# Compressed keys beside the selected branch's keys: one key tile, shared score matmuls, and the first loads in another order

## The chip, the cores and the metric

The kernel runs on one core of a Trainium2 chip. The metric is the device time in microseconds of one execution. A core has TensorE (PE in the rows; PEld is its weight loading), VectorE (DVE), ScalarE (ACT), GpSimd (POOL) and SyncE (SP, which here issues the DMAs). Each engine works through its own list of instructions in a fixed order, and waits on semaphores for the others.

## What is computed

One decoder layer on 1024 tokens of width 1024, in float32. One input projection feeds two groups of heads; their outputs are joined, projected, added to the input and normalised, and a SwiGLU feed-forward part with a second normalisation follows. The part that matters here is the sparse-attention group, with 8 heads in 2 key groups. Each head has three branches that share the query, and a gate weighs each branch's output:

```python
s_c = einsum('btghd,bngd->btghn', q, kc) * scale          # compressed: 63 keys, one per 16 tokens
p_cmp = masked_softmax(s_c, mask_c)                        # key n is seen from token 16 n + 31 on
o_cmp = einsum('btghn,bngd->btghd', p_cmp, vc)
...
s = einsum('bqghd,bqgkd->bqghk', q_blk, kg) * scale        # selected blocks of 64 tokens
s = s - slopes * dist                                      # linear distance penalty
p = masked_softmax(s, dist >= 0)
...
o = gates[..., 0:1] * o_cmp + gates[..., 1:2] * o_sel + gates[..., 2:3] * o_win
```

There are 16 blocks and 16 are selected, so the selected branch is plain causal attention over all keys up to the query. The window branch sees 512 tokens back.

## The kernel before

**Numbers.** A float32 operand is split into a high and a low part (`split`, lines 78 to 82: a cast on ScalarE, a subtraction on VectorE or GpSimd), and a product is three matmuls (`mm3`, lines 113 to 117). Score matmuls use another form: the 64 features of a head and their low part are stacked on the 128 rows, so that a score is two matmuls, with the high part of the query and then the low part as weights (L303, L304).

**Stages.** First the projections that the compressed branch and the selected branch's keys need (128 columns of `w_in` each, loaded as `w_t[0]`, `w_t[1]`, `w_t[2]`), with `x` transposed in eight tiles (`xT[hf, kp]`: token half `hf`, two of the eight 128-row blocks of the width in each). For each width block `k`, three `mm3` follow one another, one into each of three PSUM banks. Then queries, values, gates, and the compressed keys (`compress`, `compress_out`: the keys of group `g` land in a tile `kcc[g]` of 64 columns). Then attention: four phases, one for each pair of sparse heads (`nsa(0)` to `nsa(3)`), then phases of differential attention, then the output projection, the feed-forward part and the stores.

**A phase of a pair of heads** has 16 units: for each block `i` of 128 queries the selected branch (kind 0, `128 (i + 1)` keys) and the window branch (kind 1, up to 640 keys). A unit has a front and a back. The front makes the scores of both heads `a` (`scores`: pieces of at most 512 columns, each in one of the two banks of the PSUM tag S; VectorE reads a piece once, adds the distances, scales, and keeps the row minimum, L307), then exponentials on ScalarE with the sum of each row (L320), reciprocals (L400) and one multiplication by reciprocal and gate on GpSimd (L401). The back transposes the result on TensorE (L339), splits it, and multiplies by the values into the PSUM tag O (L408 for the compressed branch, L416 and L418 for the other two). The back of a unit comes after the front of the next one (`look` is 1), and pieces of later projections ("fillers") are put between.

**The compressed branch** is done for four blocks and both heads at once, in `cmp_front` (lines 357 to 380), at blocks 0 and 4 of each phase: 16 matmuls of 64 columns into one bank, a copy to SBUF, the causal mask by an affine select on GpSimd, minimum, subtraction, exponentials, sum, reciprocal and the gated multiplication, over a 128x512 tile `pc`.

**What sets the order.** The code is written against priorities (backs and fillers are put later, by `BACK_LATER` and `FILL_LATER`), and a scheduler that simulates the engines writes the fixed order of each engine's list when the kernel is built. DMAs leave SP's queue in order; a DMA that has to wait holds those behind it. SBUF tiles are named slots: slot 0 and slot 1 hold the keys of group 0 for the selected and the window branch, slots 6 and 7 those of group 1.

## Time and profile before

| | |
|---|---|
| runs timed | 1336.2, 1337.75, 1339.09 us; median 1337.75 us |
| the profiled execution | 1335.19 us, of which the span of the rows is 1333.5 us |
| TensorE busy | 1305.0 us, 98% of the span |
| VectorE, ScalarE, GpSimd busy | 918.9, 638.3 and 468.9 us |
| the four phases of sparse heads | 89.0 to 413.8 us of the span |

The span runs from the first to the last instruction of the program. Matmuls overlap in the rows (one of 512 columns shows some 0.4 us, and the next starts 0.23 us after it), so what a matmul costs is read from the starts of neighbours, not from its length.

### The profile page before, as it was taken

The page shows a single profiled execution, that of the slowest core. Times are in us where ns is not written, and L with a number is a line of the kernel's source. Part 1 is how long each engine was busy: PE and PEld are TensorE (multiplying, and loading weights), DVE is VectorE, ACT ScalarE, POOL GpSimd, SP SyncE. Part 2 cuts the span into 40 slices and gives each one's busy share as a digit, 9 for nine tenths or more (in the row PEclk, how much of TensorE's full clock was granted, in tenths as well). Part 3 has the DMA queues.
Part 4 walks back from the last instruction along what each step waited for, and adds up shares of the span by engine and source line. Part 5 has one row for each costly group of instructions (what it writes and reads, how often), then busy time and mean ns, then how long its engine had stood idle before and what let it go on. Part 6 is the DMA issues. An engine that isn't in the chain of part 4 may idle for free.

```text
span 1333.5 us, 20339 instructions
## 1 busy us (share of the span) xinstructions
PE 1305.0 (98%) x7018; PEld 1116.4 (84%) x7018; DVE 918.9 (69%) x1882; ACT 638.3 (48%) x1293; POOL 468.9 (35%) x464
## 2 busy tenths in 40 slices
PE   8999999999999998999999999999999999999997
PEld 6898998888888887878878888888888888888886
DVE  5546767868799456675687668777677777555587
ACT  5336676767787447653345233333333335533330
POOL 5415354453455336554522233223213232000072
PEclk9999999999999999999999999999999999999999
DMA  9411021120211215523212656555455549868541
GB/s 348 140 29 50 19 61 48 31 62 24 62 33 46 72 48 159 181 96 118 103 64 81 219 192 242 180 181 190 156 201 182 190 158 317 291 202 286 192 173 63
DMA packets 86695, 183.12 MB, mean 137 GB/s; under 512 B 10560, under 2 KB 19136, under 8 KB 86464
## 3 DMA queue, kind: packets, MB, share of 16 engines
q1 hardware_dynamic: 86592, 181.82, 41.4%
q8 instruction: 55, 0.90, 0.3%
q14 instruction: 48, 0.39, 0.1%
HBM read 116.18 MB, written 57.15 MB: 130 GB/s over the span
## 4 chain that ended last, share of the span: by engine, by line
PE 88%; DVE 4%; DMA 3%; ACT 1%; issue 1%; POOL 1%; SPq 0%; POOLq 0%; DVEq 0%; ACTq 0%
PE psM L115 10%; PE psM L117 10%; PE psM L116 10%; PE psT L117 6%; PE psT L115 6%; PE psT L116 6%; PE psS L117 6%; PE psS L115 6%; PE psS L116 5%; PE psT L339 4%; PE psS L303 3%; PE psS L304 3%; PE psO L418 2%; PE psO L472 2%; PE psO L416 2%; PE psO L117 2%
## 5 line engine op out<-in xcount | busy, mean ns | idle before, releaser
L320 ACT ACTIVATE t<-t,m 128x128 f32<-128x128 f32 (+7 forms) x192 | 144.2, 752 | 73.6 <-DVE m L307 69.0
L401 POOL TENSOR_SCALAR t<-t,r,gates 128x640 f32<-128x640 f32 (+7 forms) x128 | 100.0, 783 | 152.0 <-DVE r L400 104.0
L115 PE MATMUL psM<-big,w 128*128 128x512 f32 x304 | 121.4, 399 | 2.0 <-ACT w L80 2.0
L117 PE MATMUL psM<-big,w 128*128 128x512 f32 x304 | 121.1, 399 | 0.0
L116 PE MATMUL psM<-big,w 128*128 128x512 f32 x304 | 120.2, 396 | 0.0
L303 PE MATMUL psS<-slot,q 128*128 128x320 f32 (+5 forms) x288 | 106.4, 372 | 7.4 <-DVE m L307 5.4
L971 POOL TENSOR_TENSOR half<-half,half 128x512 f32<-128x512 f32 x22 | 33.3, 1515 | 198.7 <-ACT half L970 198.7
L82 DVE TENSOR_TENSOR pt<-psT,pt 128x512 fp32r<-128x512 f32 (+1 forms) x152 | 91.5, 613 | 12.4 <-ACT pt L80 11.5
L304 PE MATMUL psS<-slot,q 128*128 128x320 f32 (+5 forms) x288 | 95.2, 333 | 0.0
L307 DVE CUSTOM_DVE_ANT_0 t<-psS,dsel 128x512 f32<-128x512 f32 (+5 forms) x128 | 67.7, 535 | 34.1 <-PE psS L304 30.2
L80 ACT CAST pt<-psT 128x512 fp32r<-128x512 f32 (+1 forms) x152 | 76.8, 527 | 26.5 <-PE psT L339 14.1
L82 DVE TENSOR_TENSOR op<-op 128x1024 fp32r<-128x1024 f32 x44 | 60.7, 1385 | 38.9 <-ACT op L80 35.7
L339 PE MATMUL psT<-ident,t 128*128 128x128 f32 x528 | 83.8, 273 | 1.5 <-DVE pt L82 1.3
L82 DVE TENSOR_TENSOR big<-slot,big 128x1024 fp32r<-128x1024 f32 (+1 forms) x53 | 65.3, 1239 | 27.6 <-ACT big L80 27.5
L80 ACT CAST big<-slot 128x1024 fp32r<-128x1024 f32 (+1 forms) x53 | 54.0, 1034 | 61.6 <-DVE slot L963 55.2
L80 ACT CAST op<-op 128x1024 fp32r<-128x1024 f32 x44 | 45.9, 1051 | 65.2 <-DMA op<-t_d 57.2
L418 PE MATMUL psO<-pt,slot 128*128 128x256 f32 x264 | 73.2, 298 | 0.7 <-DVE pt L82 0.6
L975 POOL TENSOR_TENSOR half<-half,half 128x512 f32<-128x512 f32 x22 | 36.4, 1657 | 101.8 <-DVE half L974 101.7
L416 PE MATMUL psO<-pt,slot 128*128 128x256 f32 x264 | 71.7, 289 | 0.6 <-ACT pt L80 0.6
L303 PEld LDWEIGHTS psS<-slot,q 128*128 128x128 f32 x288 | 54.4, 189 | 17.7 <-DVE m L307 12.9
L339 PEld LDWEIGHTS psT<-ident,t 128*128 128x128 f32 x528 | 62.5, 140 | 7.7 <-issue 1.4
L115 PEld LDWEIGHTS psM<-big,w 128*128 128x128 f32 x304 | 57.2, 188 | 12.6 <-ACT w L80 2.7
(372 smaller groups left out, 3957.0 us busy)
## 6 DMA issues: line engine op xcount, KB each, us to landing
a_d<-slot SPq DMA_DIRECT2D x77, 256.0 KB, 3.1
t_d<-slot SPq DMA_DIRECT2D x77, 256.0 KB, 2.3
q<-q SPq DMA_DIRECT2D x48, 256.0 KB, 3.0
slot<-in_w_up_dram SPq DMA_DIRECT2D x22, 512.0 KB, 3.9
slot<-in_w_down_dram SPq DMA_DIRECT2D x22, 512.0 KB, 3.9
op<-a_d SPq DMA_DIRECT2D x44, 256.0 KB, 3.1
op<-t_d SPq DMA_DIRECT2D x44, 256.0 KB, 3.8
big<-a_d SPq DMA_DIRECT2D x33, 256.0 KB, 2.9
```

What stands on the lines that cost most here:

```text
L80: nc.scalar.copy(hi, src)
L82: eng.tensor_sub(lo, src, hi.bitcast(F32))
L115: nc.tensor.matmul(acc, lhsT=ah, rhs=bh, start=first, stop=False, skip_group_check=more)
L116: nc.tensor.matmul(acc, lhsT=ah, rhs=bl, start=False, stop=False, skip_group_check=more)
L117: nc.tensor.matmul(acc, lhsT=al, rhs=bh, start=False, stop=last, skip_group_check=more)
L303: nc.tensor.matmul(ps[:, :w], lhsT=q[0], rhs=k[:, ks], start=True, stop=False)
L304: nc.tensor.matmul(ps[:, :w], lhsT=q[1], rhs=k[:, ks], start=False, stop=True)
L320: nc.scalar.activation(t[:, :width], t[:, :width], AF.Exp, bias=m, scale=-1.0, accum_out=r)
L339: nc.tensor.transpose(tp[:rows, n * P:(n + 1) * P], s, ident)
L401: nc.gpsimd.tensor_scalar(ts[a][:, :width], ts[a][:, :width], r[:, a:a + 1], gates[:, i, gc:gc + 1], op0=ALU.mult, op1=ALU.mult)
L416: nc.tensor.matmul(po[:, :256], lhsT=v, rhs=pt[:, 0, n * 256:(n + 1) * 256], start=False, stop=False)
L418: nc.tensor.matmul(po[:, :256], lhsT=v, rhs=pt[:, 1, n * 256:(n + 1) * 256], start=False, stop=last)
```

## The change

1. The compressed keys no longer have a tile of their own. The key tile of the selected branch (slots 0 and 6) grows from 1024 to 1088 columns; the first 64 hold the compressed keys. `cmp_front` goes. In a selected unit the first score piece covers the 64 compressed keys and the first part of the selected keys, with the same two matmuls.
2. VectorE reads that first piece twice: 64 columns with a new distance tile `dcmp` (zero, or huge where the key is not yet to be seen), the rest as before. The compressed softmax is now done for each unit and head: an exponential over 64 columns, four reciprocals in one instruction, one multiplication on GpSimd.
3. Pieces are cut anew: `n` pieces for 64 + width columns, in multiples of 32. Block 3 (576 columns) now has two pieces instead of one, and block 7 (1088) three instead of two.
4. The first loads are cut in halves and put in the order in which the first matmuls take them, and the low parts of the first halves of all three weights are made on VectorE.

```diff
@@ scores @@
-            n = (width + 511) // 512
-            w = width // n
+            c = NC if cmp else 0
+            n = (c + width + 511) // 512
+            w = -(-(c + width) // (32 * n)) * 32
+            part, at = width - (n - 1) * w, 0
+            m0 = None
             for h in range(n):
                 ps = ps_s()
-                ks = slice(k0 + h * w, k0 + (h + 1) * w)
-                nc.tensor.matmul(ps[:, :w], lhsT=q[0], rhs=k[:, ks], start=True, stop=False)
-                nc.tensor.matmul(ps[:, :w], lhsT=q[1], rhs=k[:, ks], start=False, stop=True)
...
+                ks = slice(k0 + at, k0 + at + part + c)
+                nc.tensor.matmul(ps[:, :c + part], lhsT=q[0], rhs=k[:, ks], start=True, stop=False)
+                nc.tensor.matmul(ps[:, :c + part], lhsT=q[1], rhs=k[:, ks], start=False, stop=True)
+                if c:
+                    k0 += c
+                    nc.vector.tensor_tensor_reduce(out=cmp[0], in0=ps[:, :c], in1=cmp[1], scale=slope, scalar=3.0e38,
+                                                   op0=ALU.add, op1=ALU.min, accum_out=cmp[2])
+                m1 = m if h == n - 1 else pa.tile([P, 1], F32, tag="m0", name="m0", bufs=4)
+                nc.vector.tensor_tensor_reduce(out=t[:, at:at + part], in0=ps[:, c:c + part],
+                                               in1=dist[:, at:at + part], scale=slope,
                                                scalar=3.0e38 if h == 0 else m0, op0=ALU.add, op1=ALU.min,
-                                               accum_out=m if h == n - 1 else m0)
+                                               accum_out=m1)
+                at, part, c, m0 = at + part, w, 0, m1
@@ nsa_units @@
-            def cmp_front(hf):
...
                 def front():
-                    if i % 4 == 0 and kind == 0:
-                        cmp_front(i // 4)
...
                     for a in range(2):
-                        scores(q_of(qt, i, a), K[kind], j0 * P, width, dist, sl[a], m[:, a:a + 1], ts[a])
-                        exps(ts[a], width, m[:, a:a + 1], r[:, a:a + 1])
+                        ms, rs = ([t[:, n:n + 1] for n in (a, 2 + a)] for t in (m, r))
+                        cmp = (pc[:, a, :], dcmp[:, 56 - 8 * i:56 - 8 * i + NC], ms[1]) if kind == 0 else None
+                        scores(q_of(qt, i, a), K[kind], j0 * P, width, dist, sl[a], ms[0], ts[a], cmp)
+                        exps(ts[a], width, ms[0], rs[0])
+                        if kind == 0:
+                            exps(pc[:, a, :], NC, ms[1], rs[1])
+                    nr = 2 if kind else 4
+                    nc.vector.reciprocal(r[:, :nr], r[:, :nr])
                     for a in range(2):
-                        gc = heads[a] * 3 + 1 + kind
-                        nc.vector.reciprocal(r[:, a:a + 1], r[:, a:a + 1])
-                        nc.gpsimd.tensor_scalar(ts[a][:, :width], ts[a][:, :width], r[:, a:a + 1],
-                                                gates[:, i, gc:gc + 1], op0=ALU.mult, op1=ALU.mult)
+                        for n, t in ((1 + kind, ts[a][:, :width]), (0, pc[:, a, :] if kind == 0 else None)):
+                            if t is not None:
+                                gc = heads[a] * 3 + n
+                                c = a if n else 2 + a
+                                nc.gpsimd.tensor_scalar(t, t, r[:, c:c + 1], gates[:, i, gc:gc + 1],
+                                                        op0=ALU.mult, op1=ALU.mult)
@@ the first loads @@
-        for k in range(2):
-            cs = slice(k * 512, (k + 1) * 512)
-            nc.sync.dma_start(raw_x[:, cs], xT[0, 0][:, cs])
-            nc.sync.dma_start(raw_w[:, cs], w_t[0][:, cs])
-            for raw, t in ((raw_x, xs[0, 0]), (raw_w, w3[0])):
-                split(raw[:, cs], t[0][:, cs], t[1][:, cs])
-        w3.append(load_split(w_t[1], *w_tiles(), land=slot(8, F32), l_eng="pool", pieces=2))
-        w3.append(load_split(w_t[2], t_tile(), t_tile(), land=slot(9, F32), l_eng="pool", pieces=2))
...
+        piece(xT[0, 0], raw_x, xs[0, 0], 0)
+        for n in range(3):
+            piece(w_t[n], raw_w[n], w3[n], 0)
+        piece(xT[0, 0], raw_x, xs[0, 0], 1)
+        load_x(0, 1, 2)
+        for n in range(3):
+            piece(w_t[n], raw_w[n], w3[n], 1, "pool" if n else "dve")
```

`piece` loads one half of a tile and splits it.

The first DMAs in SP's list, before (128x512 is half of a tile):

```order
L663 DMA slot_107<-in_xT_dram 128x512
L664 DMA w<-in_w_t_dram 128x512
L663 DMA slot_107<-in_xT_dram 128x512
L664 DMA w<-in_w_t_dram 128x512
L89 DMA slot_125<-in_w_t_dram 128x512 x2
L89 DMA slot_134<-in_w_t_dram 128x512 x2
L89 DMA slot_142<-in_xT_dram 128x1024
```

and after:

```order
L663 DMA slot_106<-in_xT_dram 128x512
L663 DMA w<-in_w_t_dram 128x512
L663 DMA slot_114<-in_w_t_dram 128x512
L663 DMA slot_115<-in_w_t_dram 128x512
L663 DMA slot_106<-in_xT_dram 128x512
L92 DMA slot_132<-in_xT_dram 128x512 x2
L663 DMA w<-in_w_t_dram 128x512
L663 DMA slot_114<-in_w_t_dram 128x512
L663 DMA slot_115<-in_w_t_dram 128x512
```

The first halves of the second and third weights move from places 5 and 7 to places 3 and 4, the second half of the first `x` tile from 3 to 5, and the next `x` tile comes ahead of the second halves of all weights.

TensorE's list at the end of the first `cmp_front`, before (`kcc0` are the compressed keys of group 0, `q_458` and `q_459` the queries of the two heads, `slot0` the selected keys):

```order
L365 MATMUL psS_843<-kcc0_86,q_459 128x64
L366 MATMUL psS_843<-kcc0_86,q_459 128x64
L303 MATMUL psS_876<-slot0_230,q_458 128x128
L304 MATMUL psS_876<-slot0_230,q_458 128x128
L116 MATMUL psM_923<-big_171,q_406 128x512
```

and after, at the same place:

```order
L313 MATMUL psS_854<-slot0_236,q_464 128x192
L314 MATMUL psS_854<-slot0_236,q_464 128x192
L313 MATMUL psS_861<-slot0_236,q_465 128x192
L314 MATMUL psS_861<-slot0_236,q_465 128x192
L119 MATMUL psM_905<-big_173,q_412 128x512
```

The matmuls of 64 columns are gone, and those of block 0's selected keys have 192 columns instead of 128. In the whole list there are 96 matmuls fewer.

VectorE's list in the selected unit of block 7 of the first phase, before (rows ending in 128x1 read the minimum out; `psS_1740` and `psS_1745` are the two banks of the first head):

```order
L307 ISA t_1738,m0_1743<-psS_1740,dsel_90 128x512
L307 ISA m0_1743 128x1
L400 RECIPROCAL r_1645<-r_1645 128x1
L424 TENSOR_TENSOR tmp_1639<-psO_1506,tmp_1639 64x256
L82 TENSOR_TENSOR pt_1685<-psT_1680,pt_1685 128x512
L82 TENSOR_TENSOR pt_1700<-psT_1695,pt_1700 128x512
L307 ISA t_1738,m_1736<-psS_1745,dsel_90,m0_1743 128x512
```

and after:

```order
L317 ISA pc_1729,m_1725<-psS_1730,dcmp_90 128x64
L317 ISA m_1725 128x1
L320 ISA t_1727,m0_1734<-psS_1730,dsel_88 128x256
L320 ISA m0_1734 128x1
L393 RECIPROCAL r_1635<-r_1635 128x2
L422 TENSOR_TENSOR tmp_1629<-psO_1490,tmp_1629 64x256
L360 TENSOR_TENSOR pt_1665<-psT_1662,pt_1665 64x256
L320 ISA t_1727,m0_1739<-psS_1736,dsel_88,m0_1734 128x384
L320 ISA m0_1739 128x1
L85 TENSOR_TENSOR pt_1674<-psT_1669,pt_1674 128x512
L85 TENSOR_TENSOR pt_1689<-psT_1684,pt_1689 128x512
L320 ISA t_1727,m_1725<-psS_1741,dsel_88,m0_1739 128x384
```

The first bank is now read by two instructions before it is free, and the head's scores come in three pieces instead of two.

## Rows read from the trace of the kernel before

**Rows 1.** The page, part 1: busy time, share of the span, instructions.

```profile
PE 1305.0 (98%) x7018; PEld 1116.4 (84%) x7018; DVE 918.9 (69%) x1882; ACT 638.3 (48%) x1293; POOL 468.9 (35%) x464
```

**Rows 2.** Busy time by stretch: PE, PEld, DVE, ACT, POOL, clock, DMA share, GB/s.

```profile
5.80:15.10 9.30, 6.70 (x24) 3.96 (x24) 4.48 (x5) 6.39 (x9) 8.08 (x23) 1.00 1.00 363
15.10:89.00 73.90, 73.90 (x448) 65.87 (x446) 36.47 (x74) 26.36 (x72) 21.23 (x18) 1.00 0.45 162
89.00:171.50 82.50, 81.65 (x559) 74.83 (x559) 58.05 (x186) 50.25 (x125) 32.47 (x39) 1.00 0.15 38
171.50:252.00 80.50, 79.38 (x554) 71.51 (x552) 60.48 (x198) 57.64 (x140) 37.90 (x44) 1.00 0.18 47
252.00:332.00 80.00, 78.72 (x513) 70.18 (x511) 58.95 (x183) 54.31 (x130) 36.81 (x43) 1.00 0.18 47
332.00:413.80 81.80, 79.87 (x562) 71.58 (x560) 70.34 (x237) 64.05 (x157) 38.75 (x48) 1.00 0.20 50
```

**Rows 3.** Waits of PE and PEld, 89 to 414: total us, times, longest.

```profile
PE psS L303 <- DVE m L307: 2.2, 6, 0.6
...
PEld psS L303 <- DVE m L307: 6.3, 16, 1.1
```

**Rows 4.** PE in order of time from 252 us: start us, length us, instruction.

```profile
253.06 0.28 PE L366 MATMUL psS<-kcc,q 128*128 128x64 f32 x1
...
254.51 0.37 PE L418 MATMUL psO<-pt,slot 128*128 128x256 f32 x1
...
255.30 0.39 PE L115 MATMUL psM<-big,w 128*128 128x512 f32 x1
...
257.14 0.40 PE L117 MATMUL psM<-big,w 128*128 128x512 f32 x1
```

**Rows 5.** What uses the tile pc: length ns min/median/max, first and last start.

```profile
L374 ACT ACTIVATE pc<-pc x16: 402/410/441, 92.5 to 376.3; 128x256 f32<-128x256 f32 x16
L368 ACT COPY pc<-psS x8: 567/586/588, 89.2 to 371.2; 128x512 f32<-128x512 f32 x8
...
L371 DVE TENSOR_REDUCE cst<-pc x8: 677/686/689, 90.6 to 373.8; 128x8 f32<-128x512 f32 x8
...
L375 DVE TENSOR_REDUCE cst<-pc x8: 628/682/687, 93.8 to 377.9; 128x8 f32<-128x512 f32 x8
```

**Rows 6.** Groups by form, 80 to 420: busy us, mean ns | idle before.

```profile
L320 ACT ACTIVATION_READ_ACCUMULATOR t<-t,m 128x1 f32 x136 | 25.8, 190 | 0.0
L400 DVE RECIPROCAL r<-r 128x1 f32<-128x1 f32 x128 | 20.0, 158 | 14.2 <-ACT t L320 12.6
...
L307 DVE DVE_READ_ACCUMULATOR2_ANT m<- 128x1 f32 x201 | 16.3, 81 | 0.0
...
L320 ACT ACTIVATE t<-t,m 128x256 f32<-128x256 f32 x18 | 9.1, 509 | 10.6 <-DVE m L307 10.6
...
L320 ACT ACTIVATE t<-t,m 128x128 f32<-128x128 f32 x18 | 7.2, 402 | 10.6 <-DVE m L307 10.4
L401 POOL TENSOR_SCALAR t<-t,r,gates 128x128 f32<-128x128 f32 x16 | 7.1, 447 | 18.5 <-DVE r L400 16.1 <-DVE gates L718 1.7 <-PE psT L339 0.6
...
L307 DVE CUSTOM_DVE_ANT_0 t<-psS,dsel 128x128 f32<-128x128 f32 x10 | 2.8, 287 | 3.1 <-PE psS L304 2.5 <-PE psT L339 0.5
```

**Rows 7.** ACT in order of time, start: the casts that end a load.

```profile
7.67 0.62 ACT L80 CAST w<-w 128x512 fp32r<-128x512 f32 x1 [1.33 <-DMA w<-in_w_t_dram]
...
9.19 0.62 ACT L80 CAST w<-slot 128x512 fp32r<-128x512 f32 x1 [0.25 <-DMA slot<-in_w_t_dram]
```

**Rows 8.** PE in order of time, start.

```profile
5.80 0.77 PE L115 MATMUL psS<-big,w 128*128 128x512 f32 x1
...
12.98 0.50 PE L115 MATMUL psS<-big,w 128*128 128x512 f32 x1 [0.74 <-ACT big L80]
```

**Rows 9.** PE in order of time, 530.9 to 536.2.

```profile
531.05 0.30 PE L303 MATMUL psS<-slot,q 128*128 128x128 f32 x1 [1.69 <-DMA q<-q]
```

**Rows 10.** Busy time by stretch, as in group 2, after that wait.

```profile
532.00:536.00 4.00, 4.00 (x24) 4.00 (x22) 0.71 (x5) 0.77 (x4) 0.73 (x2) 0.57 0.68 169
```

More of the change, by code (lines that the diff above doesn't have):

```diff
@@ L25 @@
 NCMP = 63
+NC = NCMP + 1
 WIN_BLOCKS = 5
@@ L62, in ps_m, with slot @@
         return psum.tile([P, 512], F32, tag="M", name="psM", bufs=2)
-    def slot(n, dt=F32R):
-        return slots.tile([P, 1024], dt, tag=f"slot{n}", name=f"slot{n}", bufs=1)
+    def slot(n, dt=F32R, wide=False):
+        w = 1024 + NC if n in (0, 6) else 1024
+        t = slots.tile([P, w], dt, tag=f"slot{n}", name=f"slot{n}", bufs=1)
+        return t if wide or w == 1024 else t[:, :1024]
     def w_tile(dt=F32R):
@@ L184, in layer_kernel @@
         pes = const.tile([P, 2, 16], F32, name="pes")
-        kcc = [const.tile([P, 64], F32R, name=f"kcc{g}") for g in range(2)]
         vcc = [const.tile([P, P], F32R, name=f"vcc{g}") for g in range(2)]
@@ L224, in compress_out @@
                 for g in range(2):
[L225 to L227 removed]
+                    kc = KC[g][:, :NC]
+                    nc.scalar.copy(kc[0:64, :], op[0:64, g * 64:(g + 1) * 64])
+                    nc.vector.tensor_sub(kc[64:128, :], op[0:64, g * 64:(g + 1) * 64], kc[0:64, :].bitcast(F32))
             else:
@@ L251, in layer_kernel @@
         dwin = pa.tile([P, 640], F32, tag="dwin", name="dwin", bufs=1)
+        dcmp = pa.tile([P, NC + 56], F32, tag="dcmp", name="dcmp", bufs=1)
         qscale = pa.tile([P, 12], F32, tag="qscale", name="qscale", bufs=1)
@@ L294, in q_of, with scores @@
             return q[:, c:c + P], q[:, 512 + c:512 + c + P]
[L296 to L299 removed]
+        def scores(q, k, k0, width, dist, slope, m, t, cmp=None):
+            c = NC if cmp else 0
[3 more added lines that the diff above has]
+            m0 = None
             for h in range(n):
                 ps = ps_s()
[L302 to L308 removed]
+                ks = slice(k0 + at, k0 + at + part + c)
[8 more added lines that the diff above has]
+                                               in1=dist[:, at:at + part], scale=slope,
                                                scalar=3.0e38 if h == 0 else m0, op0=ALU.add, op1=ALU.min,
[L310 removed]
+                                               accum_out=m1)
+                at, part, c, m0 = at + part, w, 0, m1
         def t_tiles(width):
@@ L355, in nsa_units @@
             state = {}
-            def cmp_front(hf):
-                pc = pa.tile([P, 2, 4, 64], F32, tag="pc", name="pc", bufs=2)
-                ps = ps_s()
-                for a in range(2):
-                    for i4 in range(4):
-                        q = q_of(qt, hf * 4 + i4, a)
-                        o = ps[:, (a * 4 + i4) * 64:(a * 4 + i4 + 1) * 64]
-                        nc.tensor.matmul(o, lhsT=q[0], rhs=kcc[g], start=True, stop=False)
-                        nc.tensor.matmul(o, lhsT=q[1], rhs=kcc[g], start=False, stop=True)
-                st = small([P, 3, 2, 4], "cst", 2)
-                nc.scalar.copy(pc.rearrange("p a i n -> p (a i n)"), ps)
-                nc.gpsimd.affine_select(pc, pc, pattern=[[0, 2], [P, 4], [-16, 64]], base=hf * 512 - 31,
-                                        channel_multiplier=1, compare_op=ALU.is_ge, fill=BIG)
-                nc.vector.tensor_reduce(st[:, 0], pc, axis=AX.X, op=ALU.min)
-                nc.gpsimd.tensor_sub(pc, pc, st[:, 0].unsqueeze(3).to_broadcast([P, 2, 4, 64]))
-                for a in range(2):
-                    nc.scalar.activation(pc[:, a], pc[:, a], AF.Exp, scale=-sl[a])
-                nc.vector.reduce_sum(st[:, 1], pc, axis=AX.X)
-                nc.vector.reciprocal(st[:, 1], st[:, 1])
-                gc = gates[:, hf * 4:hf * 4 + 4, 6 * p:6 * p + 6].rearrange("p i (a c) -> p a i c", c=3)[:, :, :, 0]
-                nc.vector.tensor_mul(st[:, 2], st[:, 1], gc)
-                nc.gpsimd.tensor_mul(pc, pc, st[:, 2].unsqueeze(3).to_broadcast([P, 2, 4, 64]))
-                state[hf] = pc
             def make(i, kind):
@@ L406, in back @@
                         state["po"] = po = ps_o()
-                        ptc = transposed([state[i // 4][:, a, i % 4, :] for a in range(2)], rows=64)
+                        ptc = transposed([ts[2][:, a, :] for a in range(2)], rows=64)
                         nc.tensor.matmul(po[:, :256], lhsT=vcc[g], rhs=ptc[:, 0, :256], start=True, stop=False)
```

35 lines of the change are left out of this document (20 added, 15 removed).

## The prediction

> **What bounds the kernel now.** I read the page's first part first: TensorE is busy for 98% of the span [rows 1]. So a change here is worth what it takes off TensorE's list, or off the few waits in it; work on another engine counts only where TensorE comes to wait for it. Then the busy times by stretch [rows 2], which say where such waits are. From 15.10 to 89.00 us TensorE is busy for all 73.90 us. In the four phases of sparse heads it is busy for 319.6 of 324.8 us (sum of the four rows), while VectorE is busy for 247.8, ScalarE for 226.3 and GpSimd for 145.9. In the first 9.30 us after the first real matmul it is busy for 6.70, with DMA at 1.00. Third, the waits of TensorE in the phases [rows 3]: the largest is a score matmul or its weight load that waits for VectorE to free a bank of tag S, 6 and 16 times, 2.2 and 6.3 us. That is the wait which the change can feed.
>
> **The change part by part.**
>
> *Matmuls taken away.* `cmp_front` runs twice in each of four phases, 16 matmuls each, 128 in all. Their cost is their spacing: from the one at 253.06 to the matmul behind the last at 254.51 there are 13 steps in 1.45 us, 0.1115 us each [rows 4]. 128 x 0.1115 = 14.3 us.
>
> [...]
>
> *Columns given back.* The same 64 columns now ride on the selected units' matmuls. Eight 512-column matmuls take 257.14 - 255.30 = 1.84 us [rows 4], 0.23 us each, so 64 columns cost 0.23/8 = 0.029 us if cost goes with columns. 4 phases x 8 blocks x 2 heads x 2 matmuls = 128 times 0.029 = 3.7 us. For block 0 (128 becomes 192 columns) the cost may be nothing, since 64 columns with their weight load already take 0.11; that takes at most 0.5 off, and I take 3.4.
>
> *Pieces added.* Blocks 3 and 7 get one piece more: 2 blocks x 4 phases x 2 heads x 2 = 32 matmuls more, with no more columns. 128 - 32 = 96 fewer, as the lists say. The pieces have at least 256 columns, whose stream at 0.23 us for 512 is 0.115 us and so covers the 0.11 us that a weight load sets [rows 4]. I take 0; if none is covered, 32 x 0.11 = 3.5 us. Sum for TensorE: -14.3 + 3.4 = -10.9, between -14.3 and -6.5.
>
> *The first loads.* Between 5.80 and 15.10 us there are 24 matmuls [rows 2], at 0.23 us 5.5 us of work, so 3.8 us are lost; the last gap ends at 12.98 with the cast of the second `x` tile, after 0.74 us [rows 8]. Until then the second and third weights came 5th and 7th, the second `x` tile 9th. In the new order the first half of the third weight is the 4th transfer. The 4th transfer's cast begins at 7.67 now [rows 7], the bytes ahead of it are the same, so the third bank's first matmul comes at 7.67 + 0.62 = 8.3. Six matmuls (1.4 us) can run between 5.8 and 8.3; 1.1 us is lost. The 6th transfer's cast is at 9.19 [rows 7], so halves land every 0.76 us, and each half of an `x` tile feeds nine matmuls, 2.1 us: no wait behind 8.3. The gain is 3.8 - 1.1 = 2.7 us. It lasts only if nothing later needs a load sooner than it comes; no wait stands between 15.10 and 89.00, and the total bytes are the same. Bounds 0 and 3.8.
>
> *VectorE.* Taken away: two reductions of 0.69 and 0.68 us, 8 times [rows 5], 11.0 us; 64 reciprocals of 0.158 [rows 6], 10.1 us. Added: 64 reads of 64 columns. A read of 128 columns takes 0.287 us [rows 6]; 64 cost between half of that and all of it, I take 0.215, as most of a short instruction is fixed, and the minimum read out 0.081: 64 x 0.296 = 18.9 us. 16 pieces more at about 0.285 (the fixed part and the minimum): 4.6 us. Sum +2.4 us in 325: no load to speak of.
>
> *The wait for banks.* What changes is when a bank comes free: 64 first pieces are held 0.296 us longer, and behind each wait the second head's scores, the fillers and the back of the unit before, since TensorE's list is fixed. Bounds: 0, if there is always a matmul between, and 18.9 + 4.6 = 23.5 us, if TensorE stands for all of it. Today 22 of 201 reads [rows 3, 6] release a TensorE that stands, 11%. I take 11% of 23.5 = 2.6 us, near the lower end, because the rows lie there.
>
> *ScalarE.* Taken away: 8 copies of 0.586 and 16 exponentials of 0.410 [rows 5], 11.2 us. Added: 64 exponentials of 64 columns with their sums. 128 columns take 0.402 and 256 take 0.509 [rows 6], so 64 take about 0.349, and the sum read out 0.190: 64 x 0.539 = 34.5 us. Net +23.3 us. I cost this at nothing on the path: ScalarE idles for 98.5 us of the phases [rows 2]. The price without that cover is in the rivals.
>
> *GpSimd.* 64 multiplications of at most 0.447 us [rows 6], 28.6 us, against three passes over `pc` taken away 8 times. It idles for 179 us of the phases [rows 2], mostly for reciprocals [rows 6], so 0. What is later: a reciprocal now waits for four sums, and the compressed part, which the back transposes first, is multiplied among the last. A unit's back runs after the next unit's front, some 5 us of TensorE (82 us by 16 units), and the delay is two exponentials, 1.1 us. If that cover were gone, 32 units x 1.1 = 35 us.
>
> *Sum.* 1335.19 (the profiled execution's own time: its span of 1333.5 and 1.7 around it) - 10.9 - 2.7 + 2.6 = 1324.2. The median of the runs lies 2.6 above that execution, so I expect 1326.8, say **1327**: 0.8% less. 0.2% (2.7 us) is about what a measurement of this kernel can tell from no change.
>
> **The rivals.**
>
> *A. ScalarE becomes the bound, and it is slower.* ScalarE's list also holds the casts of the transposed blocks that TensorE's value matmuls wait for; an exponential put ahead of such a cast delays it. The price is the 23.3 us above. The change gives 13.6, so it ends slower by 0.2% once over 16.3 of the 23.3 (70%) fall on TensorE; with all of it and no wait for banks the time is 1337.75 - 13.6 + 23.3 = 1347. For it: in the fourth phase ScalarE is busy for 64.05 of 81.80 us [rows 2], and with a quarter of 23.3 more in 79 us it would be at 88%. Against it: 98.5 us of idle time in the phases, so that 64 remain when the phases are 11 us shorter. Chance 0.08.
>
> [...]
>
> *B. More stalls, half the gain.* Banks and exponentials together cost TensorE 6 to 11 us instead of 2.6: the three pieces of block 7 need a third bank where there are two. Time 1337.75 - 13.6 + 8.5 = 1332.6, between 1330 and 1335. For it: in the fourth phase VectorE is busy for 86% [rows 2]. Against it: the lists are written around these waits by a scheduler, which puts fillers there. Chance 0.20.
>
> *C. It takes back what it gives.* The start's gain is lost at a later load, and the stalls eat the matmuls: within 2.7 us of 1337.75. Chance 0.10.
>
> *D. More than forecast.* [...] Chance 0.12.
>
> **How the numbers follow.** The forecast, 1323 to 1330, has 0.50; D, below 1323, 0.12; B 0.20; C 0.10; A 0.08. The range from 1319 to 1335 holds the forecast, D but for a little, and B, some 0.8. Faster by over 0.2% (below 1335): 0.82. Within 0.2%: 0.10. Slower: 0.08.
>
> **What would show it.** No rows of 64 columns with `kcc`; score rows of 320, 352, 416 and 480 columns at the same 0.23 us per 512. TensorE's gaps before 15 us are down to one, and each later stage begins some 2.7 us sooner. The first phase begins 2.7 us sooner and the four phases together are about 8 us shorter. ScalarE's busy time is up by about 23 us and VectorE's by less than 3. The wait of scores for VectorE grows by 2 to 3 us. [...]

## The result and the profile after

The changed kernel takes 1330.42 us (median of four runs, 1329.40 to 1331.26) and the kernel before, run beside it, 1336.97 us (1335.98 to 1339.09). The ratio is 0.9949, with a 95% interval from 0.9931 to 0.9966: 6.6 us or 0.51% less. The forecast was 1327, with a range of 1319 to 1335. The time is inside the range, but where the forecast's own stretch (1323 to 1330) ends and rival B begins.

First the page's busy times, as [rows 1] of before:

```profile
PE 1301.0 (98%) x6922; PEld 1106.2 (83%) x6922; DVE 914.5 (69%) x1949; ACT 649.7 (49%) x1398; POOL 467.4 (35%) x504
```

There are 96 matmuls fewer, as forecast, and TensorE is still the engine that never rests. So the question is where the time between the stages' ends went. These are starts of the same matmuls in both timelines of TensorE:

| matmul | before, us | after, us | lead, us |
|---|---|---|---|
| first of the compression | 56.40 | 52.77 | 3.6 |
| last value matmul of the compressed branch (end of the four phases) | 413.80 | 405.75 | 8.0 |
| first transpose behind the differential heads | 635.96 | 631.04 | 4.9 |
| last of the program | 1324.95 | 1320.38 | 4.6 |

The lead grows to 8.0 us, and then 3.1 us of it are lost in the differential heads, whose code is the same. The windows of after by stage show both (columns as in [rows 2]; the four phases are the third to sixth row, the differential heads the last):

```profile
5.80:8.31 2.51, 2.20 (x8) 1.35 (x8) 1.54 (x3) 1.57 (x3) 2.15 (x12) 1.00 0.97 353
15.10:84.15 69.05, 69.05 (x420) 61.70 (x419) 31.86 (x72) 26.18 (x69) 19.50 (x14) 1.00 0.49 174
84.15:164.50 80.35, 79.42 (x542) 72.81 (x541) 52.09 (x192) 51.50 (x147) 30.88 (x46) 1.00 0.16 39
164.50:244.50 80.00, 78.97 (x538) 70.41 (x536) 60.27 (x221) 61.64 (x168) 38.17 (x54) 1.00 0.19 47
244.50:323.80 79.30, 77.80 (x479) 66.25 (x478) 56.43 (x205) 56.11 (x154) 38.07 (x54) 1.00 0.19 47
323.80:405.80 82.00, 79.85 (x538) 69.28 (x538) 68.94 (x247) 67.44 (x188) 38.87 (x59) 1.00 0.21 47
405.80:631.00 225.20, 216.65 (x1292) 188.25 (x1292) 141.66 (x393) 120.57 (x313) 108.82 (x106) 0.99 0.36 104
```

The phases last 321.65 us, only 3.1 less than before. In them TensorE waits as follows (total us, times, longest; first for matmuls, then for weight loads), to be laid beside [rows 3]:

```profile
PE psS L313 <- DVE m L320: 3.2, 10, 0.7
PE psT L353 <- DVE pt L85: 0.9, 3, 0.5
...
PEld psS L313 <- DVE m L320: 7.5, 22, 0.7
PEld psT L353 <- issue: 3.4, 11, 0.7
PEld psO L416 <- DVE pt L85: 2.9, 11, 0.3
PEld psS L313 <- PE psT L353: 1.8, 6, 0.6
PEld psS L313 <- PE psS L314: 1.5, 2, 0.9
```

Added up as in [rows 3], the wait of scores for VectorE is 10.7 us where it was 8.5, the 2 to 3 us more that were forecast. But these rows count an event twice: each of the ten waits of a matmul here stands again, and longer, at its weight load, and so did all six of before. By the weight loads alone the wait is 7.5 us where it was 6.3. They also miss waits: with those that are put down to TensorE's own instructions (the last two rows), weight loads of scores stand idle for 10.9 us in all, where before there were none but the 6.3.

A wait also shows as a wider step from one matmul to the next. So I added up, for every matmul of the phases, the usual step of its width, an estimate from the starts of neighbours (0.108 us up to 240 columns, 0.145 for 320, 0.229 for 512, in proportion between; the medians before are 0.112 for 64 columns, 0.109 for 128, 0.119 for 256, 0.148 for 320 and 0.231 for 512). That sum fell from 303.35 to 293.70 us. What the phases lose beyond it rose from 21.4 to 27.9 us, by 6.5. The idle time of all weight loads there, whatever it is put down to, says the same: it rose from 16.3 to 22.6 us, by 6.3, and 4.6 of that stand ahead of scores. This loss has to be explained.

The new instructions on the other engines (view of tile `pc`: count, shortest, median and longest ns, first and last start):

```profile
L317 DVE CUSTOM_DVE_ANT_0 pc<-psS,dcmp x64: 185/217/226, 84.5 to 393.7; 128x64 f32<-128x64 f32 x64
L334 ACT ACTIVATE pc<-pc,m x64: 332/347/362, 84.8 to 395.6; 128x64 f32<-128x64 f32 x64
L334 ACT ACTIVATION_READ_ACCUMULATOR pc<-pc,m x64: 185/190/202, 85.1 to 395.9; 128x1 f32 x64
L399 POOL TENSOR_SCALAR pc<-pc,r,gates x64: 384/394/415, 90.8 to 402.1; 128x64 f32<-128x64 f32 x64
```

Their durations are what the prediction said: 0.217 us for a read (0.215), 0.347 and 0.190 for an exponential and its sum (0.349 and 0.190), 0.394 on GpSimd (at most 0.447). ScalarE's busy time in the phases rose by 10.4 us though (the sum of the four rows, 226.3 before and 236.7 after), not by 23.3. ScalarE's timeline of after says why:

```profile
241.09 0.19 ACT L334 ACTIVATION_READ_ACCUMULATOR t<-t,m 128x1 f32 x1
241.19 0.34 ACT L334 ACTIVATE pc<-pc,m 128x64 f32<-128x64 f32 x1
241.43 0.19 ACT L334 ACTIVATION_READ_ACCUMULATOR pc<-pc,m 128x1 f32 x1
241.52 0.57 ACT L83 CAST pt<-psT 128x512 fp32r<-128x512 f32 x1
```

Neighbours overlap by 0.1 us each, so an exponential and its sum take 0.33 us of the engine (241.19 to 241.52) and not 0.54: 21 us for 64 of them, against about 9 taken away when the same 0.1 is taken off each. The load was overpriced, on the safe side. So no price of an instruction explains the loss; an order or a wait must.

### The profile page after: what moved, and what is told of

It is laid out like the page before. It is cut to its first block, busy times and chain, and to the rows that moved or that the text cites. A ratio compares the mean times of both kernels' runs of the same rounds, so it can differ in the third digit from the quotient of the medians.

```text
span 1328.9 us, 20439 instructions
## 1 busy us (share of the span) xinstructions
PE 1301.0 (98%) x6922; PEld 1106.2 (83%) x6922; DVE 914.5 (69%) x1949; ACT 649.7 (49%) x1398; POOL 467.4 (35%) x504
## 4 chain that ended last, share of the span: by engine, by line
PE 90%; DVE 4%; ACT 2%; DMA 2%; issue 2%; SPq 0%; POOLq 0%; DVEq 0%; POOL 0%; ACTq 0%
PE psM L118 10%; PE psM L120 10%; PE psM L119 10%; PE psT L118 6%; PE psT L119 6%; PE psT L120 6%; PE psS L120 6%; PE psS L118 6%; PE psS L119 6%; PE psT L353 4%; PE psS L313 3%; PE psS L314 3%; PE psO L416 2%; PE psO L470 2%; PE psO L414 2%; PE psO L118 2%
## 5 line engine op out<-in xcount | busy, mean ns | idle before, releaser
L313 PE MATMUL psS<-slot,q 128*128 128x320 f32 (+10 forms) x304 | 113.7, 376 | 8.0 <-DVE m L320 5.3
L314 PE MATMUL psS<-slot,q 128*128 128x320 f32 (+10 forms) x304 | 99.4, 329 | 0.0
L313 PEld LDWEIGHTS psS<-slot,q 128*128 128x128 f32 x304 | 57.4, 189 | 23.1 <-DVE m L320 13.7
L320 DVE CUSTOM_DVE_ANT_0 t<-psS,dsel 128x384 f32<-128x384 f32 (+9 forms) x128 | 62.4, 493 | 16.3 <-PE psS L314 15.4
```

The source lines that it names most:

```text
L313: nc.tensor.matmul(ps[:, :c + part], lhsT=q[0], rhs=k[:, ks], start=True, stop=False)
L314: nc.tensor.matmul(ps[:, :c + part], lhsT=q[1], rhs=k[:, ks], start=False, stop=True)
```

## The experiments

Theories at the start. **Banks:** the second read and its minimum hold a bank 0.3 us longer, and TensorE waits for it. **ScalarE:** the 64 new exponentials stand ahead of casts that TensorE needs (rival A, in part). For the 3.1 us in the differential heads: **loads** (the start's gain is handed back at a later load), or **order** (the scheduler writes their list anew too).

### The two parts by themselves

```diff
@@ e1_loads_only: before, with the first loads of after @@
+        piece(xT[0, 0], raw_x, xs[0, 0], 0)
+        for n in range(3):
+            piece(w_t[n], raw_w[n], w3[n], 0)
+        piece(xT[0, 0], raw_x, xs[0, 0], 1)
@@ e2_keys_only: after, with the first loads of before @@
-        piece(xT[0, 0], raw_x, xs[0, 0], 0)
...
+            nc.sync.dma_start(raw_x[:, cs], xT[0, 0][:, cs])
+            nc.sync.dma_start(raw_w[:, cs], w_t[0][:, cs])
```

> The kernel before with only the new order of the first loads. The changed kernel's compression started 3.6 us sooner, and its time from the end of the sparse heads to the end of the differential heads was 3.1 us longer. If the loads' gain is kept, this kernel ends about 3.6 us below the kernel before, near 1333.4, and its differential phases take the 222.2 us of before. If those 3.1 us are the same gain, given back at a later load, this kernel ends within 1 us of the kernel before and its differential phases take about 225.

> The changed kernel with the old order of the first loads, so with the keys in one tile alone. If the two parts add up, it ends about 3.6 us above the changed kernel, near 1334, and its differential phases still take about 225 us, 3 more than before. If the start's gain was given back later anyway, it ends within 1 us of the changed kernel, near 1330.5, with differential phases of about 222.

The loads alone: 1333.51 us, ratio 0.9974 (0.9964 to 0.9984), 3.5 us less than before. The keys alone: 1334.38 us, 0.9978 (0.9968 to 0.9988), some 4 us more than the changed kernel. The parts add up, and the loads are worth about 3.5 us at the end. The differential heads took 222.6 us with the loads alone and 226.2 us with the keys alone. So the loads theory falls: the start's gain is kept.

### Matmuls of their own for the compressed keys

```diff
-                ks = slice(k0 + at, k0 + at + part + c)
-                nc.tensor.matmul(ps[:, :c + part], lhsT=q[0], rhs=k[:, ks], start=True, stop=False)
-                nc.tensor.matmul(ps[:, :c + part], lhsT=q[1], rhs=k[:, ks], start=False, stop=True)
+                for lo, hi in ((0, c), (c, c + part)) if c else ((0, part),):
+                    ks = slice(k0 + at + lo, k0 + at + hi)
+                    nc.tensor.matmul(ps[:, lo:hi], lhsT=q[0], rhs=k[:, ks], start=True, stop=False)
+                    nc.tensor.matmul(ps[:, lo:hi], lhsT=q[1], rhs=k[:, ks], start=False, stop=True)
```

> The changed kernel with the 64 columns of compressed keys scored by matmuls of their own again, in the same bank ahead of the selected piece; the softmax stays per block. If a short matmul costs its spacing, 0.11 us, against 0.029 for 64 columns more in a longer one, 128 of them cost 10.9 us and the time is near 1341. If the folding itself is worth little, because the longer matmuls wait for VectorE in any case, it stays below 1334.

1337.24 us, ratio 1.0001 (0.9992 to 1.0009): 6.8 us above the changed kernel, between the two expectations. The usual steps of the phases' matmuls add up to 304.54 us, 10.84 more than in the changed kernel. That is the forecast's 10.9 priced once more by width, and no test of it; the test is the time. The stretch from the compression to the end of the phases is 5.5 us longer than in the changed kernel (358.5 and 353.0), because the loss beyond the steps is 5.2 less, 22.7 us. So about half of what the folding gives was handed back as loss. Whether the short matmuls only fill waits that the folding leaves empty isn't separated here.

### One part of the new softmax less

```diff
@@ e3_no_short_exps @@
-                        if kind == 0:
-                            exps(pc[:, a, :], NC, ms[1], rs[1])
-                    nr = 2 if kind else 4
+                    nr = 2
...
-                                c = a if n else 2 + a
+                                c = a
@@ e4_one_read: one read of all columns of a piece @@
-                if c:
-                    k0 += c
-                    nc.vector.tensor_tensor_reduce(out=cmp[0], in0=ps[:, :c], in1=cmp[1], scale=slope, scalar=3.0e38,
-                                                   op0=ALU.add, op1=ALU.min, accum_out=cmp[2])
```

> The changed kernel without its 64 exponentials of 64 columns and their sums (the compressed scores go on as they are, multiplied with the selected branch's reciprocal; masked ones are 0): ScalarE has 34 us less to do, the matmuls and VectorE's reads are the same. If the 6.5 us that the sparse phases lose beyond the spacing of their matmuls come from banks that VectorE frees later, the time stays within 2 us of the changed kernel's, near 1330. If they come from ScalarE, whose casts stand behind the new exponentials, it falls by 5 to 7 us, to about 1324.

> The changed kernel with one VectorE read for the whole first piece of a selected unit in place of two (64 columns and the rest): the tiles of the selected units and the distance table are widened by 64 columns, and both parts share one minimum, so the compressed part's mask is left out and its keys and exponentials are scaled down to stay finite. It takes 64 reads of 0.216 us and 64 minimum read-outs of 0.081 off VectorE, adds 64 columns to another, and frees the bank some 0.25 us sooner. If TensorE waits for banks because of the second read, the time falls by 3 to 6 us, to 1325 to 1327; if ScalarE's exponentials alone cost the time, it stays within 1.5 us of 1330.4.

Without the exponentials (so without a compressed softmax): 1326.25 us, 0.9916 (0.9903 to 0.9929), 4.2 us less than the changed kernel, between the two theories. From the compression to the end of the phases it takes 349.3 us where the changed kernel takes 353.0.

With one read (and without the compressed part's mask): 1326.28 us, 0.9923 (0.9911 to 0.9935). That looks like the banks theory's number, but it is not in the place where the theory puts it: the same stretch takes 353.4 us, and its loss is 27.4 us, as in the changed kernel. Scores wait longer for VectorE than before, in the phases of this kernel:

```profile
PE psS L312 <- DVE m L315: 3.0, 11, 0.6
...
PEld psS L312 <- DVE m L315: 10.5, 29, 0.8
```

The gain is in the differential heads (220.5 us against 225.3), which have no such read. So the second read isn't what the phases lose by, and a total alone would have misled.

### GpSimd's order

The back of a selected unit transposes the compressed probabilities of both heads first. The changed kernel makes them last: GpSimd multiplies selected, compressed, selected, compressed.

```diff
@@ e6_pc_first @@
-                    for a in range(2):
-                        for n, t in ((1 + kind, ts[a][:, :width]), (0, pc[:, a, :] if kind == 0 else None)):
+                    for n in (0, 1) if kind == 0 else (2,):
+                        for a in range(2):
+                            t = ts[a][:, :width] if n else pc[:, a, :]
@@ e9_pc_last @@
+                    for n in (1, 0) if kind == 0 else (2,):
```

> The changed kernel with GpSimd's multiplications in the order in which the back reads them: both compressed parts first, then the two selected ones. If the back's first transposes wait for the compressed part (PEld waits for GpSimd's pc are 0.3 us in the sparse phases after), the time falls by under 1 us and stays within 2 us of 1330.4; if the delay of the compressed part is what was lost, it falls by 3 us or more.

> The changed kernel with GpSimd's multiplications the other way round: both selected parts first, then the two compressed ones, which the back transposes first. The theory of order: the later the compressed part is ready, the later a unit's back comes in TensorE's list, and the more score pieces stand directly behind another score there (36 in the sparse phases before, 53 in the changed kernel, 30 with the compressed parts first), where a wait for a bank is covered by nothing. Then there are more than 53 here, the sparse phases lose more than the changed kernel's 28 us, and the time is 1 to 5 us above it, 1331 to 1336. If the 6 us that the other order gained were luck of the planner, the time lies anywhere within 3 us of 1330.4 and the count does not follow the order.

Compressed first: 1324.04 us, ratio 0.9909 (0.9895 to 0.9924), 6 us less than the changed kernel. Under 1 us had been expected if the wait of 0.3 us in the rows were all; it is the other case, that the delay of the compressed part costs time. But only 3.0 us of it lie between the compression and the end of the phases; 3.3 us lie in the differential heads, whose code this edit doesn't touch. Compressed last: 1330.81 us, 0.9960 (0.9947 to 0.9972), the same as the changed kernel, where the theory of order asked for more. The reason shows when the trace is asked what this order moves. From VectorE's first read of a unit's compressed scores to the end of the second head's product takes 9.10 us on average over the 32 units in the changed kernel and 9.10 with the compressed parts last (the second one was the last of the four in either order), and 7.67 with them first. So the run was no test of a later product; it is one of a product that isn't moved, and nothing moved.

### Early all along

```diff
@@ e10_pc_early: on top of e6_pc_first @@
-                        exps(ts[a], width, ms[0], rs[0])
                         if kind == 0:
                             exps(pc[:, a, :], NC, ms[1], rs[1])
-                    nr = 2 if kind else 4
-                    nc.vector.reciprocal(r[:, :nr], r[:, :nr])
+                        exps(ts[a], width, ms[0], rs[0])
+                    for n in (2, 0) if kind == 0 else (0,):
+                        nc.vector.reciprocal(r[:, n:n + 2], r[:, n:n + 2])
```

> The changed kernel with the compressed parts first all along: their exponentials ahead of the selected ones on ScalarE, a reciprocal of their own (32 more on VectorE, 0.16 us each, 5 us in all), and first on GpSimd. The theory of order: 30 pieces or fewer behind another score and a time at or below that of GpSimd's order alone, 1321 to 1324.5. If VectorE's load counts, the 5 us more of it show, and the time is 1325 to 1328.

> The changed kernel once more, unchanged, on the chip of the two above, as what they are compared with: 1330.4, within 1 us.

1320.74 us, ratio 0.9885 (0.9866 to 0.9903): 15.9 us less than before, and a full 10.7 less than the changed kernel on the same chip (1331.44 us, 0.9963, 0.9950 to 0.9977). This version computes the same and beats both kernels, with 32 instructions more on VectorE. In the profiles, 5.6 us of the gain lie between the compression and the end of the phases and 4.6 in the differential heads (225.3 and 220.7 us). Three orders are changed here at once, on ScalarE, VectorE and GpSimd; only GpSimd's was run alone. Its GpSimd at block 7 of the second phase, against the same unit of the changed kernel. First the timeline of the changed kernel (start, length, engine, instruction, idle time before it and who ended it); VectorE read this unit's compressed scores at 236.0:

```profile
246.38 1.19 POOL L399 TENSOR_SCALAR t<-t,r,gates 128x1024 f32<-128x1024 f32 x1 [6.87 <-DVE r L393]
247.56 0.40 POOL L399 TENSOR_SCALAR pc<-pc,r,gates 128x64 f32<-128x64 f32 x1
247.93 1.22 POOL L399 TENSOR_SCALAR t<-t,r,gates 128x1024 f32<-128x1024 f32 x1
249.10 0.41 POOL L399 TENSOR_SCALAR pc<-pc,r,gates 128x64 f32<-128x64 f32 x1
```

And of the version with the compressed parts early, which read them at 235.6:

```profile
241.21 0.76 POOL L399 TENSOR_SCALAR pc<-pc,r,gates 128x64 f32<-128x64 f32 x2 [1.93 <-DVE r L393]
244.09 1.20 POOL L399 TENSOR_SCALAR t<-t,r,gates 128x1024 f32<-128x1024 f32 x1 [2.12 <-DVE r L393]
```

GpSimd stood for 6.87 us until one reciprocal had all four sums, and the second compressed product was done at 249.51, 13.5 us behind the read. In the other version it was done at 241.97, 6.4 us behind. What that does to TensorE shows at block 7 of the third phase. The changed kernel's timeline, where the second head's scores come:

```profile
322.52 0.39 PE L313 MATMUL psS<-slot,q 128*128 128x320 f32 x1
322.75 0.31 PE L314 MATMUL psS<-slot,q 128*128 128x320 f32 x1
322.90 0.27 PE L353 MATMUL psT<-ident,pc 128*64 128x128 f32 x1
322.96 0.45 PE L313 MATMUL psS<-slot,q 128*128 128x384 f32 x1
323.25 0.34 PE L314 MATMUL psS<-slot,q 128*128 128x384 f32 x1
323.82 0.42 PE L313 MATMUL psS<-slot,q 128*128 128x384 f32 x1 [0.24 <-DVE m L320]
324.08 0.34 PE L314 MATMUL psS<-slot,q 128*128 128x384 f32 x1
324.50 0.42 PE L313 MATMUL psS<-slot,q 128*128 128x320 f32 x1
324.76 0.31 PE L314 MATMUL psS<-slot,q 128*128 128x320 f32 x1
325.27 0.42 PE L313 MATMUL psS<-slot,q 128*128 128x320 f32 x1 [0.21 <-DVE m L320]
325.52 0.31 PE L314 MATMUL psS<-slot,q 128*128 128x320 f32 x1
```

Five pieces with one transpose between them take 3.2 us, from 322.52 to 325.72 where the next matmul starts, for 1.7 us of usual steps: there are two banks, and VectorE's read of 384 columns takes 0.609 us (groups by form) where the two matmuls take 0.35. The matmuls' rows mark 0.45 us of it as idle time. The rows of their weight loads mark 1.41 us, nearly all of the 1.5 that are lost:

```profile
323.79 0.19 PEld L313 LDWEIGHTS psS<-slot,q 128*128 128x128 f32 x1 [0.53 <-PE psS L314]
324.50 0.19 PEld L313 LDWEIGHTS psS<-slot,q 128*128 128x128 f32 x1 [0.41 <-DVE m L320]
325.27 0.19 PEld L313 LDWEIGHTS psS<-slot,q 128*128 128x128 f32 x1 [0.47 <-DVE m L320]
```

In the version with the compressed parts early, the back of an earlier unit stands between such pieces:

```profile
322.04 0.34 PE L313 MATMUL psS<-slot,q 128*128 128x384 f32 x1
322.22 0.34 PE L314 MATMUL psS<-slot,q 128*128 128x384 f32 x1
322.40 0.28 PE L414 MATMUL psO<-pt,slot 128*128 128x256 f32 x1
322.72 0.39 PE L416 MATMUL psO<-pt,slot 128*128 128x256 f32 x1
322.94 0.28 PE L414 MATMUL psO<-pt,slot 128*128 128x256 f32 x1
...
323.44 0.42 PE L313 MATMUL psS<-slot,q 128*128 128x384 f32 x1
```

Over all units, with the number of score pieces whose first matmul follows a score matmul directly, and what TensorE loses there beyond the usual steps. The times from VectorE's read go to the end of the second compressed product and to the first value matmul of the unit's back:

| kernel | read to second product, mean us | read to value matmul, mean us | pieces behind a score | lost there, us | compression to end of phases, us |
|---|---|---|---|---|---|
| before | | 16.0 | 36 | 3.7 | 357.4 |
| after | 9.10 | 17.8 | 53 | 7.2 | 353.0 |
| e9, compressed last | 9.10 | 17.5 | 52 | 7.0 | 352.7 |
| e2, keys only | 9.72 | 18.3 | 52 | 6.4 | 351.7 |
| e4, one read | 9.07 | 18.0 | 44 | 6.8 | 353.4 |
| e5, matmuls of their own | 8.87 | 17.2 | 38 | 5.2 | 358.5 |
| e3, no short exponentials | 8.97 | 16.6 | 35 | 5.4 | 349.3 |
| e6, compressed first | 7.67 | 16.6 | 30 | 2.8 | 350.0 |
| e10, early all along | 5.93 | 15.4 | 27 | 2.6 | 347.4 |

TensorE does not stand for the product itself: in the changed kernel the value matmul comes 8.7 us behind it on average and 3.3 at the least, and the weight loads of the phases wait for it for 0.3 us. What moved is the back itself, 1.8 us later behind the read than before. By and large, a back that comes sooner goes with fewer pieces behind a score and less lost there. With the product sooner (e6, e10) the scheduler puts the back sooner. In e10 the selected products come no sooner than in the changed kernel (8.7 us behind the read in both), so it is the compressed ones that count. That the back is the link was read from these traces; no run moved it alone. The pieces behind a score hold 3.5 of the 6.5 us.

e10 keeps all 64 exponentials, so their load on ScalarE is no bound. Without them (e3) the back comes as soon as in e6 with hardly an earlier product; why the scheduler puts it there is open.

One rival is left. The selected scores of blocks 3 and 7, which have a piece more, lose some 6.1 us beyond their usual steps where they lost 2.8. At block 7 this falls in e10 (from 3.2 to 1.8), at block 3 it doesn't (2.9 and 2.8). No run has the keys in one tile with the old number of pieces.

### The differential heads

> A control: the changed kernel with the planner's lead for filler work at 1.20 in place of 1.25, so the same work in another order. If the 3.1 us that the unchanged differential phases take longer come from their new order by chance, their length changes by some us here, in either direction, with no change in what they compute; if they come from something that the change brings with it, they stay at about 225 us and the time within 1.5 us of 1330.4.

> The same control with the lead at 1.30. By chance: differential phases between some 221 and 228 us, and a time that follows them; by the change: about 225 us and within 1.5 us of 1330.4.

```diff
-AHEAD = 1.25
+AHEAD = 1.2
```

1330.24 us (0.9955, 0.9942 to 0.9967) and 1330.54 us (0.9958, 0.9946 to 0.9971) at 1.20 and 1.30, with differential heads of 223.4 and 225.4 us. But these are no controls. At 1.20 the instructions of all four engines stand in the order of the changed kernel, place by place, so this is the changed kernel run again; at 1.30 TensorE's list differs in 50 of 6922 places, none of them in this stretch. So neither is a test of the chance theory.

The traces of the other kernels settle more. In this stretch TensorE's list is the same, by operation, tile and shape, in the kernel before and in e1. It is another one in the changed kernel, and the same as there in e2, e3, e5, e7, e8, e9 and the repeat (e11). The old list takes 222.2 and 222.6 us, the new one 223.4 to 226.2, with a mean of 224.8 over eight profiles. So the scheduler does write this stretch's list anew for the keys in one tile, as the theory of order says, and in the mean the new list takes 2.4 us more. About 0.9 of that is no loss, but eight transposes of sparse units (0.108 us each) that the new list has behind the matmul where the stretch begins. Some 0.6 is a drop of the clock (below), which seven of the eight profiles have, and one of the two of the old list: an estimate, 7/8 less 1/2 of the 1.7 us that 3.4 us at a granted clock of 0.50 lose. The 0.9 that is left is less than executions of one list differ by. e4, e6 and e10 have lists of their own, with 220.5, 222.0 and 220.7 us. The rows show one part of what sets them apart. Windows and the wait of the changed kernel there:

```profile
523.00:527.00 4.00, 1.88 (x15) 1.67 (x14) 0.68 (x5) 0.68 (x4) 0.00 (x0) 0.95 1.05 279
527.00:531.00 4.00, 4.00 (x25) 4.00 (x24) 0.79 (x5) 2.29 (x8) 0.73 (x2) 0.63 0.44 92
...
PE psS L313 <- DMA q<-q: 2.1, 1, 2.1
```

TensorE waits 2.1 us for queries that a DMA moves, and is granted a clock of 0.63 in the second window, as in [rows 9, 10]. The version with the compressed parts early, in the stretch that answers to it:

```profile
515.00:519.00 4.00, 3.74 (x32) 3.54 (x32) 3.69 (x14) 1.39 (x7) 2.75 (x4) 1.00 0.88 284
519.00:523.00 4.00, 4.00 (x35) 4.00 (x34) 2.51 (x11) 3.38 (x11) 1.48 (x4) 1.00 0.59 116
```

No wait of that kind stands in its rows, and none in those of e4 and e6. These three have the shortest differential heads. In all other kernels, the one before among them, TensorE waits 1.4 to 2.6 us for those queries. So the wait of [rows 9] is real, and an edit in the sparse heads makes it go or stay by the order that the scheduler writes for the rest; why the queries are in time in those three is open.

The drop of the clock is another matter. The granted clock is 0.50 from 532.1 to 535.5 us before and from 526.6 to 530.0 after, 3.4 us both times. Of the ten profiles with the wait it stands behind it in four (before, after, e2 and e8). In e1 and e7 this stretch has none. In e3, e5, e9 and the repeat one stands some 30 us ahead of the wait; in the repeat TensorE has waited twice for VectorE before it, at 490.89 and 492.26 us, for 0.77 and 0.70:

```profile
494.00:498.00 4.00, 3.92 (x16) 2.92 (x16) 3.87 (x10) 3.02 (x8) 0.97 (x2) 0.57 0.31 97
```

The changed kernel, e7 and the repeat have one and the same list, with 225.3, 223.4 and 225.2 us. So the drop comes and goes with the execution, also behind the same waits, and goes with some 1.8 us here. The profiles of before and after have one drop each, so the 3.1 us between these two don't hang on it. But e1, with the list of before and no drop, takes as long as before with one, so part of the 3.1 us is the luck of one execution.

## Why the prediction came out as it did

The time is inside the range, but it is rival B's time and not the forecast's. The gain was forecast at 11.0 us and came as 6.6, and the kernel before ran 0.8 us under the base from which the forecast was added up, which brings the time nearer by luck. In the two profiled executions the lead at the end is 4.6 us. Point by point:

- **Matmuls, -10.9.** Right as a price of steps. The usual steps fall by 9.65 us in the phases. The first `cmp_front` stood ahead of them, and 1.3 us are saved there. Undoing the folding made the kernel 6.8 us slower, so not all of the price reaches the time. The step of the short matmuls goes with their weight loads: from 253.20 to 254.50 us before, 14 matmuls and 14 weight loads fill PE and PEld, 1.30 us each, 0.11 us from one start to the next in both. The least gain that was given, 6.5, doesn't follow from the terms beside it (14.3 - 3.7 - 3.5 = 7.1). The 32 matmuls of added pieces cost nothing in these sums by the way in which they are priced; beyond that price, the 32 of block 3 (288 columns) lose 3.0 us.
- **First loads, -2.7.** Right in kind, and 0.9 too small: 3.6 us at the compression and 3.5 us in the time of e1. In the two profiles with the changed kernel's own list (e7 and the repeat) the compression starts another 0.7 and 0.9 us sooner, so 0.9 is what executions of one list differ by. The third bank's first matmul starts at 8.31, as forecast (8.3), and one gap is left, 0.31 us.
- **VectorE, ScalarE and GpSimd, loads.** Durations right to 2%, GpSimd's within its bound. Of VectorE's 0.217 us for 64 columns an estimated 0.147 is fixed, from 0.287 for 128 [rows 6]. As loads they were summed without the overlap of neighbours: in the phases ScalarE rose by 10.4 us and not by 23.3, and VectorE fell by 10.1 where it was to rise by 2.4 [rows 2]. The sum for VectorE also left out two short instructions of `cmp_front` (L376 and L378), 4.4 us in all.
- **Wait for banks, +2.6.** The 22 waits from which the price was read are 16, since the six of matmuls stand again among the weight loads: 16 of 201 would have given 1.9 us. Counted once, the same rows grew by 1.2 us. The loss grew by 6.5; 3.4 of it is idle time ahead of scores that stands under other releasers. The longer hold wasn't its cause (e4).
- **ScalarE and GpSimd at 0.** This is the step that failed. It said that a unit's back runs some 5 us of TensorE later and that the delay is 1.1 us, so that it is covered. In the kernel before, a unit's second selected product ended 7.2 us behind VectorE's first read of the unit, and the back's first value matmul came at 16.0. Now the second compressed product, which the back needs first, ends at 9.1 (9 to 15 us at blocks 4 to 7): the reciprocal waits for four sums, and the product stands behind a long selected product. That is 1.9 us later, and the back moved by about as much, to 17.8. So the cover was longer than was said and held in the execution; what wasn't priced is that the scheduler puts the whole back later, and leaves scores to follow scores. Without that delay (e10), the phases lose about what they lost before: the steps leave 22 us, against 21.4 before and 27.9 in the changed kernel.
- **Rivals.** B's stalls of 6 to 11 us came true at their lower end (6.5). B's reason, the added pieces, may hold up to half of it (blocks 3 and 7 above) and wasn't run alone. A didn't come true: ScalarE is no bound. D didn't come true: the wait for the queries and the lower clock behind it [rows 9, 10] stayed in the changed kernel (2.1 us of wait, and 3.4 us at a granted clock of 0.50, by estimate 1.7 us lost), and the wait went in e4, e6 and e10. The differential heads took 3.1 us more in the two profiles, which no step had, since their code is the same; their list is not, and over all profiles of the two lists the difference is 2.4, 0.9 of it moved work.

## What to carry to other kernels

When a piece of work is moved into another unit, ask who reads its result first, and make it first on every engine that it passes: the exponential, the reciprocal and the product. An engine that is idle a quarter of the time can still deliver late: ScalarE is busy for 236.7 of the phases' 321.65 us in the changed kernel, and with its order changed beside VectorE's and GpSimd's (e10) the second compressed product came 5.93 us behind VectorE's read on average and not 9.10. Read a loss of TensorE from the steps between matmuls and from the idle time of all weight loads, whatever it is put down to, and count an event once. Look stage by stage: e4 had the right total for the wrong reason. Where a scheduler writes the order, code that wasn't touched can move by some 2 us, a third of what this change was worth; so compare the lists first, and don't take a kernel for a control whose list is the same.

## What was not expected of the hardware

At block 7 of the third phase, the changed kernel's waits for banks are marked almost in full at the weight loads and only in part at the matmuls: of 1.5 us lost over five pieces, 1.41 us stand in the rows of weight loads and 0.45 in those of matmuls. ScalarE's neighbours overlap by 0.1 us in the rows (241.09 to 241.52 us), so that a short exponential with its sum costs 0.33 us and not the 0.54 of its two durations. And the drop of the granted clock, from 1.00 to 0.50 for 3.4 us before and after, stood behind the wait for the queries (1.4 to 2.6 us) in four of the ten profiles with such a wait; three executions of one list had it there, elsewhere, and not at all.
